# Attention steps of a head pair given to the next pair's stages from its first step on, and rope parts transposed ahead of the queries

## The chip, the cores and the metric

The kernel runs on one core of a Trainium2 chip. The metric is the device time of one execution in microseconds (us), and the time of a kernel is the median of several executions. The engines are named as in the profile: PE is TensorE (matmuls and transposes), PEld its weight loads, DVE is VectorE, ACT is ScalarE, POOL is GpSimd and SP is SyncE, which issues most DMAs.

## The reference

The program computes a two-layer encoder trunk on 512 tokens of width 1024: an mLSTM layer with a memory attention, then a multi-head latent attention layer (8 heads) with a memory attention. The change lies in the second layer. Cut to what matters:

```python
def shared_kv(...):                        # 8 heads, 128 plain + 64 rope columns
    c_kv, k_pe = split_cols(h @ w_kv_a, [KV_LORA, QK_ROPE])
    kv = (rmsnorm(c_kv, kv_lat_norm) @ w_kv_b).reshape(b, s, 8, 128 + 128)
    k = concat(kv[..., :128], broadcast(k_pe)); k = rmsnorm(k, k_gain)
    return concat(k[..., :128], rope(k[..., 128:])), kv[..., 128:]

def mla_layer(...):
    q = rmsnorm((rmsnorm(q_lat) @ w_q_up).reshape(b, s, 8, 192), q_gain)
    q = concat(q[..., :128], rope(q[..., 128:]))
    for j in range(4):                     # blocks of 128 queries
        sc = q_j @ k[: (j + 1) * 128].T * scale     # chunk-causal mask
        attn_j = softmax(sc) @ v[: (j + 1) * 128]
    y_b = attn * silu(z)                   # z: gate columns of h @ w_in
    return x + concat(y_b, y_mem) @ w_out
```

## The kernel before

Every product of two f32 operands is made of three matmuls on split operands: each operand is written as a high part and a low part (`split`, or in `load` for weights: ACT writes the high part at L130, DVE the rest at L131), and `prod` issues the high weight with both parts of the activation (L157), then the low weight with the high part (L162).

The second layer goes over four pairs of heads, p = 0 to 3. `b_pair(p)` is a generator of 14 steps, which are called m0 to m13 here:

- m0 to m3, `b_kv`: keys and values of token tile t0 to t3 (six matmuls of 512 columns each). DVE copies the keys out (L928), ACT the values.
- m4 to m7, `b_q`: queries of token tile t0 to t3 (nine matmuls of 384 columns each).
- m8 to m10 and m11 to m13, `b_z(p, 0)` and `b_z(p, 1)`: the gate of one head, in two halves of twelve matmuls of 512 columns, and a step with the SiLU (ACT tanh L200, DVE multiply L201). After each of these six steps `b_T` makes one transposed operand out of `todo`: k0, k1 (plain keys of head 0 and 1), q0, q1 (plain queries), kr, qr (the rope parts of both heads). Four PE transposes go into a PSUM tile `tp` (L952 for plain parts, L957 for rope parts). The high part is then written by ACT and the low part by DVE (L131 or L134 for plain parts; L960 and L963 for the rope parts, with a DVE cast L962 between them for the keys).

The tile `tp` is the one that all transposes share, and there are two of it:

```python
return pp.tile(list(shape), F32, tag="tp", bufs=2, name=nm("tp"))
```

The eight PSUM banks are 4 `acc`, 2 `att` and 2 `tp`. Weights have two buffers each of `wr`, `wh` and `wl`, so that a weight's split waits until the matmuls of the weight two loads earlier have read their buffer.

`b_attn(p)` is the attention of a pair, a generator of nine steps, n = 0 to 8. It goes over six units, u0 to u5: for each head the query blocks (0, 1) together, then block 2, then block 3. Step n issues the scores s of unit n (five matmuls for each block: L157 twice, L162, L1004, L1005), and the transposes t of unit n - 2 (L1018, into a `tp`, copied to the tile `e` by DVE at L1024 or, for block 2, by ACT at L1022). Steps 5 and 8 also issue the values of a head (20 matmuls at L1031) and its gated output (L346). Between scores and transposes lies the softmax on DVE and ACT (L328 to L341).

`weave(main, side, plan)` runs `main` and after its step i runs plan[i] steps of `side`. The attention of pair p runs as `side` beside the projections of pair p + 1; the attention of pair 3 runs beside the output projection. Pairs 0 and 1 are emitted in one order and then ordered on all engines by the framework's scheduler. The last `weave` (pairs 2 and 3, and the output projection) stands under `manual_schedule` for PE: there PE's order is that of the program, while the scheduler orders the other engines. Every engine goes through its own fixed list in order.

Of the kernel before, what the change touches and what calls it, by code (L numbers as in the profile page):

```python
# [40 lines left out]
def weave(main, side, plan=()):  # L41
    for i, _ in enumerate(main):
        for _ in range(plan[i] if i < len(plan) else 1):
            next(side, None)
    for _ in side:
        pass


def chain(*gens):
    for g in gens:  # L50
        yield from g
# [8 lines left out]
def trunk(ctx: ExitStack, tc: tile.TileContext, pv_d, pos_d, x_d, mem_d, memT_d, wmem_d, wg_d, wa_d, woa_d,  # L60
# [20 lines left out]
    def st(shape, tag, bufs=1, dt=F32):  # L81
        return POOLS.get(tag, sp).tile(shape, dt, tag=tag, bufs=bufs, name=nm(tag))
# [12 lines left out]
    def acc(shape=(P, 512)):  # L95
        return pp.tile(list(shape), F32, tag="acc", bufs=4, name=nm("acc"))

    def att(shape=(P, 512)):
        return pp.tile(list(shape), F32, tag="att", bufs=2, name=nm("att"))

    def tps(shape=(P, 512)):
        return pp.tile(list(shape), F32, tag="tp", bufs=2, name=nm("tp"))
# [46 lines left out]
    def prod(items, start, stop):  # L149

        left = {}
        for it in items:
            left[id(it[0])] = left.get(id(it[0]), 0) + 1
        seen = set()
        for ps, a_, w_, lhs in items:
            for x in a_:
                PE.matmul(ps, x if lhs else w_[0], w_[0] if lhs else x,  # L157
                          start=start and id(ps) not in seen, stop=False)
                seen.add(id(ps))
        for ps, a_, w_, lhs in items:  # L160
            left[id(ps)] -= 1
            PE.matmul(ps, a_[0] if lhs else w_[1], w_[1] if lhs else a_[0], start=False,  # L162
                      stop=stop and left[id(ps)] == 0)
# [159 lines left out]
    def softmax_rows(rows_, rq):  # L323

        n = len(rows_)
        mx = tiny([P, n])
        for j, ps in enumerate(rows_):
            V.tensor_reduce(mx[:, j:j + 1], ps, axis=AX.X, op=ALU.max)  # L328
        nb = tiny([P, n])
        V.scalar_tensor_tensor(out=nb, in0=mx, scalar=-1.0, in1=rq, op0=ALU.mult, op1=ALU.mult)  # L330
        pr = s2([P, 512])
        out = []
        sm = tiny([P, n])
        o = 0
        for j, ps in enumerate(rows_):
            out.append(pr[:, o:o + ps.shape[-1]])
            o += ps.shape[-1]
            A.activation(out[j], ps, AF.Exp, bias=nb[:, j:j + 1], scale=rq[:, j:j + 1], accum_out=sm[:, j:j + 1])  # L338
        V.reciprocal(sm, sm)
        for j in range(n):  # L340
            V.tensor_scalar(out[j], out[j], sm[:, j:j + 1], None, op0=ALU.mult)  # L341
        return out

    def gate_out(yT, row, ps, sz):
        y = s2()
        V.scalar_tensor_tensor(out=y, in0=ps, scalar=0.5, in1=sz, op0=ALU.mult, op1=ALU.mult)  # L346
        split(yT[0][:, row], yT[1][:, row], y)
# [557 lines left out]
    def b_z(p, c):  # L905
        d = pairs.setdefault(p, {})
        if c == 0:
            d["z"] = st([P, 2, S], ("z4", "mv")[p % 2])
        sz = d["z"]
        w = load(wb_d[8 + 2 * p + c], KT, P)  # L910
        ps = acc()
        yield from proj_T(w, hT, ps)
        silu2(sz[:, c], ps)
        yield

    def b_kv(p):
        d = pairs.setdefault(p, {})
        kns = st([P, NT, 256], "s4", 2)
        krs = s2([P, NT, P])
        d["v"] = vt = st([P, NT, 256], ("gt", "mkT")[p % 2])  # L920
        d["ks"] = kns, krs
        w = load(wkvb_d[p], 2, 512)
        ss = tiny([P, NT, 2])
        r2 = tiny([P, NT, 2])
        for t in range(NT):
            ps = acc()
            prod([(ps, lat(ckT, k, t), sub(w, slice(None), k), True) for k in range(2)], True, True)
            V.tensor_copy(kns[:, t], ps[:, 0:256])  # L928
            A.activation(vt[:, t], ps[:, 256:512], AF.Copy)
            for h in range(2):  # L930
                sqsum(kns[:, t, h * P:(h + 1) * P], ss[:, t, h:h + 1])
            if t < 3:
                yield
        V.tensor_tensor(out=ss, in0=ss, in1=sspe.unsqueeze(2).broadcast_to([P, NT, 2]), op=ALU.add)
        rpow(r2.rearrange("p a b -> p (a b)"), ss.rearrange("p a b -> p (a b)"), 1.0 / 192, EPS, 8)
        k4 = kns.rearrange("p t (h c) -> p t h c", h=2)
        V.tensor_tensor(out=k4, in0=k4, in1=r2.unsqueeze(3).broadcast_to([P, NT, 2, P]), op=ALU.mult)
        G.tensor_tensor(out=krs.rearrange("p t (h c) -> p t h c", h=2),
                        in0=kb.unsqueeze(2).broadcast_to([P, NT, 2, 64]),
                        in1=r2.unsqueeze(3).broadcast_to([P, NT, 2, 64]), op=ALU.mult)  # L940
        yield
# [48 lines left out]
    def b_attn(p):  # L990
        kn, qn, kh, qr, vt, sz, rqp = (pairs[p][n] for n in ("kn", "qn", "kr", "qr", "v", "z", "rq"))
        prs, pTs = {}, {}

        def scores(h, tiles):
            ps = acc() if p < 3 and tiles[0] == 2 else att()
            views = []
            for j, i in enumerate(tiles):
                n = (i + 1) * P
                m = max(n, 256)
                qs = slice(i * P, (i + 1) * P)  # L1000
                pt = ps[:, j * 256:j * 256 + m]
                prod([(pt, (qn[h][:, 0, qs], qn[h][:, 1, qs]), (kn[h][:, 0, :m], kn[h][:, 1, :m]), True)],
                     True, False)
                PE.matmul(pt, qr[:, h, qs], kh[:, h, :m], start=False, stop=False)  # L1004
                PE.matmul(pt, qr[:, h, qs], kl[:, h, :m], start=False, stop=True)  # L1005
                views.append(pt[:, :n])
            for v in views:
                V.memset(v[0:64, -64:], -1.0e30)
            prs[h, tiles] = softmax_rows(views, rqp[:, tiles[0]:tiles[-1] + 1, h])

        def trans(h, tiles):
            if tiles[0] == 0:
                pTs[h] = st([P, 1280], "e", 1)
            tp = tps()
            n = 0
            for i, pr in zip(tiles, prs[h, tiles]):
                for c in range(i + 1):
                    PE.transpose(tp[:, n:n + P], pr[:, c * P:(c + 1) * P], ident)  # L1018
                    n += P
            o = tiles[0] * (tiles[0] + 1) // 2 * P  # L1020
            if tiles[0] == 2:
                A.activation(pTs[h][:, o:o + n], tp[:, :n], AF.Copy)  # L1022
            else:
                V.tensor_copy(pTs[h][:, o:o + n], tp[:, :n])  # L1024

        def values(h):
            ps = att()
            for i in range(NT):
                for c in range(i + 1):
                    o = (i * (i + 1) // 2 + c) * P  # L1030
                    PE.matmul(ps[:, i * P:(i + 1) * P], vt[:, c, h * P:(h + 1) * P], pTs[h][:, o:o + P],  # L1031
                              start=c == 0, stop=c == i)
            gate_out(yT, 2 * p + h, ps, sz[:, h])

        units = [(h, tiles) for h in range(2) for tiles in ((0, 1), (2,), (3,))]
        lag = 2
        for n in range(len(units) + lag + 1):
            if n < len(units):
                scores(*units[n])
            if 0 <= n - lag < len(units):  # L1040
                trans(*units[n - lag])
            m = n - lag - 1
            if m >= 0 and m % 3 == 2:
                values(m // 3)
            yield

    def b_pair(p):
        yield from b_kv(p)
        yield from b_q(p)
        todo = [(n, h) for h in range(3) for n in "kq"]  # L1050
        for _ in chain(b_z(p, 0), b_z(p, 1)):
            yield
            b_T(p, *todo.pop(0))

    drain(b_pair(0))
    weave(b_pair(1), b_attn(0), (0,) * 5)
    x1b = []

    def residual():
        x1b.extend(load_x(x1_d, nc.sync))  # L1060
        yield from ()
# [5 lines left out]

    with tc.manual_schedule(engines={mybir.EngineType.PE}):
        weave(chain(*(b_pair(p) for p in range(2, 4)), residual(), out_proj(wob_d, yT, b_done)),
              chain(*(b_attn(p) for p in range(1, 4))), ((0,) * 5 + (1,) * 9) * 2)  # L1070


_OUTS = [((1, S, D), 'float32')]
# [101 lines left out]
```

## Time and profile before

| | |
|---|---|
| median of 3 runs | 769.12 us (769.11 to 769.58) |
| the profiled execution | 769.35 us, of which the traced span is 767.6 us |
| PE busy | 755.0 us, 98% of the span |
| PEld busy | 647.8 us, 84% |
| DVE busy | 484.1 us, 63% |
| ACT busy | 409.4 us, 53% |
| POOL busy | 106.8 us, 14% |

A share of busy time is an average over the whole span. Matmuls are pipelined and their ends are modelled, so that the duration of a row on PE is longer than the distance to the next row; the argument goes by the distances between starts. Pair 2 takes the stretch from 598.85 us of the span to 645.52, and pair 3 the one from 645.52 to 684.90; the output projection follows.

### The profile page before, as it was taken

To read this page: it belongs to the slowest core of one execution; us is meant where nothing else is said; L and a number is where in the kernel's file an instruction comes from. 1 tells how busy PE (TensorE), PEld (TensorE's weight loads), DVE (VectorE), ACT (ScalarE), POOL (GpSimd) and SP (SyncE) were. 2 spreads that over 40 slices of the span, in tenths; PEclk is the share of its full clock that TensorE was granted. 3 is DMA by queue.
4 is the path that set the end of the run, shared out by engine and by line. 5 is a ranking of instruction groups with operands and counts; after the bars stand their busy time and mean duration, and the time that the engine had idled before them with its cause. 6 is when DMAs were issued, how large, how long until landed. Compare 5 with 4: busy or idle time off the path is not lost.

```text
span 767.6 us, 10826 instructions
## 1 busy us (share of the span) xinstructions
PE 755.0 (98%) x3948; PEld 647.8 (84%) x3948; DVE 484.1 (63%) x945; ACT 409.4 (53%) x958; POOL 106.8 (14%) x159
## 2 busy tenths in 40 slices
PE   8999998999999999999999999999999999999998
PEld 6798887888888888888888887899888888888886
DVE  5743599547868836766434664566758697776422
ACT  6964557345446435536333658457856666644220
POOL 0131010010110101001001131020334230500000
PEclk9999999999999999999999999999999999999999
DMA  9523120322132222224443532121221111511241
GB/s 323 207 84 109 56 84 29 109 83 90 63 99 80 83 89 104 71 94 154 154 160 137 174 129 73 53 83 59 83 87 59 56 50 40 190 56 56 66 155 55
DMA packets 25909, 76.39 MB, mean 100 GB/s; under 512 B 3072, under 2 KB 3968, under 8 KB 25856
## 3 DMA queue, kind: packets, MB, share of 16 engines
q1 hardware_dynamic: 24144, 73.44, 28.4%
q10 hardware_dynamic: 1584, 2.25, 0.8%
q8 instruction: 31, 0.51, 0.3%
q14 instruction: 22, 0.18, 0.1%
q0 software_dynamic: 128, 0.01, 0.0%
HBM read 71.49 MB, written 4.19 MB: 99 GB/s over the span
## 4 chain that ended last, share of the span: by engine, by line
PE 85%; DVE 8%; ACT 3%; issue 1%; DMA 1%; POOL 0%; SPq 0%; ACTq 0%; DVEq 0%
PE acc L157 47%; PE acc L162 23%; PE att L157 3%; PE att L1031 2%; PE att L162 2%; DMA yTh<-in_wmem_dram 1%; DVE wl L131 1%; PE tp L1018 1%; DVE tiny L328 1%; ACT junk L187 1%; DVE kl L629 1%; ACT s L338 1%; PE tp L952 1%; PE att L715 1%; PE att L716 1%
## 5 line engine op out<-in xcount | busy, mean ns | idle before, releaser
L131 DVE TENSOR_TENSOR wl<-wr,wh 128x1024 fp32r<-128x1024 f32 (+5 forms) x117 | 136.2, 1165 | 152.9 <-ACT wh L130 126.7
L130 ACT ACTIVATE wh<-wr 128x1024 fp32r<-128x1024 f32 (+5 forms) x117 | 117.5, 1008 | 134.1 <-PE acc L157 123.8
L157 PE MATMUL acc<-wh,hTl 128*128 128x512 f32 (+3 forms) x320 | 113.3, 365 | 0.0
L157 PE MATMUL acc<-wh,hTh 128*128 128x512 f32 (+3 forms) x320 | 112.4, 367 | 0.3 <-ACT hTh L133 0.3
L157 PE MATMUL acc<-hTh,wh 128*128 128x512 f32 x256 | 101.8, 398 | 0.0
L157 PE MATMUL acc<-hTl,wh 128*128 128x512 f32 x256 | 100.3, 392 | 0.0
L157 PE MATMUL acc<-wh,yTh 128*128 128x512 f32 (+1 forms) x224 | 84.7, 382 | 0.0
L157 PE MATMUL acc<-wh,yTl 128*128 128x512 f32 (+1 forms) x224 | 84.5, 379 | 0.0
L162 PE MATMUL acc<-wl,hTh 128*128 128x512 f32 (+3 forms) x320 | 82.0, 364 | 0.0
L162 PE MATMUL acc<-hTh,wl 128*128 128x512 f32 x256 | 69.8, 392 | 0.0
L157 PEld LDWEIGHTS acc<-wh,hTh 128*128 128x128 f32 x320 | 59.1, 188 | 9.4 <-ACT hTh L133 0.6
L157 PEld LDWEIGHTS acc<-wh,hTl 128*128 128x128 f32 x320 | 59.6, 188 | 8.7 <-DVE hTl L134 0.2
L162 PEld LDWEIGHTS acc<-wl,hTh 128*128 128x128 f32 x320 | 56.5, 188 | 8.6
L162 PE MATMUL acc<-wl,yTh 128*128 128x512 f32 (+1 forms) x224 | 60.1, 378 | 0.0
L162 PEld LDWEIGHTS acc<-hTh,wl 128*128 128x128 f32 x256 | 47.6, 188 | 9.9 <-DVE wl L131 0.2
L157 PEld LDWEIGHTS acc<-hTh,wh 128*128 128x128 f32 x256 | 48.1, 188 | 9.1
L157 PEld LDWEIGHTS acc<-hTl,wh 128*128 128x128 f32 x256 | 48.2, 188 | 9.1
L157 PEld LDWEIGHTS acc<-wh,yTh 128*128 128x128 f32 x224 | 42.1, 188 | 7.2
L157 PEld LDWEIGHTS acc<-wh,yTl 128*128 128x128 f32 x224 | 42.1, 188 | 7.1
L162 PEld LDWEIGHTS acc<-wl,yTh 128*128 128x128 f32 x224 | 41.2, 188 | 7.4
L182 POOL TENSOR_SCALAR tiny<-tiny 128x8 f32<-128x8 f32 (+3 forms) x21 | 5.5, 262 | 245.1 <-ACT junk L187 68.2
L157 PE MATMUL acc<-wh,u 128*128 128x384 f32 (+1 forms) x160 | 37.8, 362 | 0.8 <-ACT u L133 0.7
(285 smaller groups left out, 1387.0 us busy)
## 6 DMA issues: line engine op xcount, KB each, us to landing
wr<-in_wa_dram SPq DMA_DIRECT2D x46, 512.0 KB, 3.2
wr<-in_wb_dram SPq DMA_DIRECT2D x16, 512.0 KB, 3.5
wr<-in_woa_dram SPq DMA_DIRECT2D x12, 512.0 KB, 3.2
wr<-in_wob_dram SPq DMA_DIRECT2D x12, 512.0 KB, 3.2
wr<-in_wmem_dram SPq DMA_DIRECT2D x8, 512.0 KB, 3.4
yTh<-in_wmem_dram SPq DMA_DIRECT2D x5, 512.0 KB, 7.3
yTl<-in_x_dram SPq DMA_DIRECT2D x4, 512.0 KB, 9.1
u<-in_x_dram SPq DMA_DIRECT2D x4, 512.0 KB, 6.2
```

What stands on the lines that cost most here:

```text
L130: A.activation(hi, src, AF.Copy)
L131: V.tensor_tensor(out=lo, in0=src, in1=hi.bitcast(F32), op=ALU.subtract)
L157: PE.matmul(ps, x if lhs else w_[0], w_[0] if lhs else x, start=start and id(ps) not in seen, stop=False)
L162: PE.matmul(ps, a_[0] if lhs else w_[1], w_[1] if lhs else a_[0], start=False, stop=stop and left[id(ps)] == 0)
L187: A.activation(j[:, :src.shape[-1]], src, AF.Square, scale=scale, accum_out=accum)
L328: V.tensor_reduce(mx[:, j:j + 1], ps, axis=AX.X, op=ALU.max)
L338: A.activation(out[j], ps, AF.Exp, bias=nb[:, j:j + 1], scale=rq[:, j:j + 1], accum_out=sm[:, j:j + 1])
L629: V.scalar_tensor_tensor(out=u[:, d:], in0=raw[:, :S - d], scalar=col("cw", (3 - d) * 16 + j), in1=u[:, d:], op0=ALU.mult, op1=ALU.add)
L715: PE.matmul(ps[:, :258], low(c, i), v[0][:, c], start=False, stop=False)
L716: PE.matmul(ps[:, :256], ph[:, blk(c, i)], v[1][:, c], start=False, stop=c == i)
L952: PE.transpose(tp[:, t * P:(t + 1) * P], main[:, t, h * P:(h + 1) * P], ident)
L1031: PE.matmul(ps[:, i * P:(i + 1) * P], vt[:, c, h * P:(h + 1) * P], pTs[h][:, o:o + P], start=c == 0, stop=c == i)
```

## The change

Two lines are changed. In all four pairs `b_T` takes its operands in another order: the rope parts kr and qr come third and fourth, ahead of both queries. For pairs 2 and 3 the plan of the last `weave` lets the attention of the pair before begin at m0 instead of m5: one step each after m0 to m4, m6, m8, m10 and m12, in place of one each after m5 to m13.

```diff
--- before.py
+++ after.py
@@ -1047,7 +1047,7 @@
     def b_pair(p):
         yield from b_kv(p)
         yield from b_q(p)
-        todo = [(n, h) for h in range(3) for n in "kq"]
+        todo = [("k", 0), ("k", 1), ("k", 2), ("q", 2), ("q", 0), ("q", 1)]
         for _ in chain(b_z(p, 0), b_z(p, 1)):
             yield
             b_T(p, *todo.pop(0))
@@ -1067,7 +1067,7 @@
 
     with tc.manual_schedule(engines={mybir.EngineType.PE}):
         weave(chain(*(b_pair(p) for p in range(2, 4)), residual(), out_proj(wob_d, yT, b_done)),
-              chain(*(b_attn(p) for p in range(1, 4))), ((0,) * 5 + (1,) * 9) * 2)
+              chain(*(b_attn(p) for p in range(1, 4))), (1, 1, 1, 1, 1, 0, 1, 0, 1, 0, 1, 0, 1, 0) * 2)
 
 
 _OUTS = [((1, S, D), 'float32')]
```

What stands on PE where pair 1 ends and pair 2 begins, before: the matmuls of the first key tile of pair 2 (`u4` are the latent's transposed tiles), then q1, the transposes of unit 5 of attention 0 and its values among kr and qr. The next row belongs to the queries of pair 2.

```order
L162 MATMUL acc_1096_5943<-wl_1084_5899,u4_877_5058 128x512 x2
L952 MATMUL tp_1069_5825<-ident_78,s4_997_5515 128x128 x4
L1018 MATMUL tp_1071_5845<-ident_78,s2_1056_5767 128x128 x4
L1031 MATMUL att_1075_5866<-e_1058_5772,gt_903_5155 128x128 x3
L957 MATMUL tp_1072_5851<-ident_78,s2_970_5434 128x128 x4
L1031 MATMUL att_1075_5866<-e_1058_5772,gt_903_5155 128x128 x4
L957 MATMUL tp_1077_5881<-ident_78,s2_998_5516 128x128 x4
L157 MATMUL acc_1110_5978<-wh_1102_5965,u4_895_5129 128x384
```

After the change, at the same place: the same first row, unit 4's transposes, qr (`tp_1069`), unit 5's transposes (`tp_1071`), q0 (`tp_1072`) and q1 (`tp_1077`), and then the first scores of attention 1.

```order
L162 MATMUL acc_1087_5904<-wl_1084_5899,u4_877_5058 128x512 x2
L1018 MATMUL tp_1068_5824<-ident_78,s2_1047_5734 128x128 x3
L1031 MATMUL att_1075_5868<-e_1058_5772,gt_903_5155 128x128 x3
L957 MATMUL tp_1069_5829<-ident_78,s2_998_5516 128x128 x4
L1031 MATMUL att_1075_5868<-e_1058_5772,gt_903_5155 128x128 x3
L1018 MATMUL tp_1071_5851<-ident_78,s2_1056_5767 128x128 x4
L952 MATMUL tp_1072_5857<-ident_78,s4_997_5515 128x128 x4
L1031 MATMUL att_1075_5868<-e_1058_5772,gt_903_5155 128x128 x4
L952 MATMUL tp_1077_5883<-ident_78,s4_997_5515 128x128 x4
L157 MATMUL att_1090_5917<-qk_1043_5704,qk_1073_5858 128x256 x2
```

Four operations with a `tp` stand behind one another there, with values between them, and q0 and q1 now lie right ahead of the scores that read them.

What DVE has at that place after the change, from the split of the next weight on: the casts and low parts of kr (from `tp_1062`), a gate multiply L201, a copy of keys L928, the low parts of qr (`tp_1069`), the copy of unit 5's transposes (`tp_1071`) and the low part of q0 (`tp_1072`).

```order
L131 TENSOR_TENSOR wl_1126_6059<-wr_1124_6056,wh_1125_6058 128x768
L962 COPY v_1063_5794<-v_1063_5794 64x512
L963 TENSOR_TENSOR kl_690_4136<-tp_1062_5793,v_1063_5794 64x512
L131 TENSOR_TENSOR yTl_629_3869<-s2_1061_5789,yTh_628_3868 128x512
L201 SCALAR_TENSOR_TENSOR mv_1031_5653<-s2_1074_5865,acc_1067_5811 128x512
L928 COPY s4_1079_5893<-acc_1087_5904 128x256
L962 COPY v_1063_5794<-v_1063_5794 64x512
L963 TENSOR_TENSOR kl_690_4136<-tp_1062_5793,v_1063_5794 64x512
L963 TENSOR_TENSOR v_1070_5830<-tp_1069_5829,v_1070_5830 64x512
L1024 COPY e_1058_5772<-tp_1071_5851 128x512
L963 TENSOR_TENSOR v_1070_5830<-tp_1069_5829,v_1070_5830 64x512
L131 TENSOR_TENSOR qk_1073_5858<-tp_1072_5857,qk_1073_5858 128x512
```

The low parts of kr stand behind a weight split, and the copy of unit 5's transposes behind them.

What stands on PE behind the first gate of pair 2 before: its last four matmuls, then scores and transposes of the attention and one transposed operand.

```order
L162 MATMUL acc_1145_6120<-hTh_626_3866,wl_1144_6117 128x512 x4
L157 MATMUL acc_1154_6183<-qk_1063_5794,qk_1070_5826 128x384 x2
L162 MATMUL acc_1154_6183<-qk_1063_5794,qk_1070_5826 128x384
L1004 MATMUL acc_1154_6183<-v_1073_5852,v_1078_5882 128x384
L1005 MATMUL acc_1154_6183<-kl_690_4136,v_1078_5882 128x384
L1018 MATMUL tp_1159_6199<-ident_78,s2_1136_6099 128x128 x4
L952 MATMUL tp_1160_6205<-ident_78,s4_1107_5975 128x128 x4
L157 MATMUL att_1163_6216<-qk_1063_5794,qk_1070_5826 128x512 x2
L162 MATMUL att_1163_6216<-qk_1063_5794,qk_1070_5826 128x512
```

After the change, at the same place: the same four matmuls, then k1 (`tp_1170`), unit 5's transposes (`tp_1173`), kr (`tp_1174`), and then the second gate.

```order
L162 MATMUL acc_1166_6209<-hTh_626_3866,wl_1165_6206 128x512 x4
L952 MATMUL tp_1170_6247<-ident_78,s4_1079_5893 128x128 x4
L1018 MATMUL tp_1173_6258<-ident_78,s2_1151_6152 128x128 x4
L957 MATMUL tp_1174_6264<-ident_78,s2_1080_5894 128x128 x4
L157 MATMUL acc_1179_6282<-hTh_626_3866,wh_1177_6278 128x512
```

Three operations with a `tp` stand directly behind one another, with no scores between them.

What DVE has for these three after the change: the split of the weight two loads on, the gate multiply, the copy of unit 5's transposes, the low part of k1, and the cast and low part of kr.

```order
L131 TENSOR_TENSOR wl_1194_6357<-wr_1192_6354,wh_1193_6356 128x1024
L201 SCALAR_TENSOR_TENSOR z4_1162_6202<-s2_1172_6255,acc_1166_6209 128x512
L1024 COPY e_1153_6157<-tp_1173_6258 128x512
L134 SCALAR_TENSOR_TENSOR qk_1171_6248<-tp_1170_6247,gg_112,qk_1171_6248 128x512
L962 COPY v_1175_6265<-v_1175_6265 64x512
L963 TENSOR_TENSOR kl_690_4136<-tp_1174_6264,v_1175_6265 64x512
```

The copy out of `tp_1173` stands behind a weight split and the gate multiply.

## Rows read from the trace of the kernel before

**Rows 1.** Stretches of pair 2 and the output projection: length, busy, clock, DMA.
```profile
core 0: us, PE busy (x) PEld busy (x) DVE busy (x) ACT busy (x) POOL busy (x), PEclk, DMA share, GB/s
598.85:645.52 46.67, 45.65 (x287) 40.44 (x286) 37.77 (x82) 29.08 (x82) 11.29 (x9) 1.00 0.18 53
...
723.00:761.00 38.00, 38.00 (x169) 31.48 (x169) 12.11 (x13) 7.00 (x7) 0.00 (x0) 1.00 0.25 83
```

**Rows 2.** Timeline of PE where it pauses in pairs 2 and 3.
```profile
start us, us, engine line op out<-in xcount [idle before <-releaser]
620.26 0.40 PE L1005 MATMUL att<-kl,v 128*128 128x512 f32 x1
620.74 0.70 PE L1018 MATMUL tp<-ident,s 128*128 128x128 f32 x3
...
625.11 0.28 PE L1005 MATMUL att<-kl,v 128*128 128x256 f32 x1
625.77 0.55 PE L1018 MATMUL tp<-ident,s 128*128 128x128 f32 x3 [0.38 <-DVE s L341]
...
632.00 0.39 PE L1005 MATMUL att<-kl,v 128*128 128x512 f32 x1
632.71 0.55 PE L1018 MATMUL tp<-ident,s 128*128 128x128 f32 x3 [0.32 <-DVE e L1024]
...
651.08 1.47 PE L157 MATMUL acc<-wh,u 128*128 128x384 f32 x6
652.38 0.51 PE L162 MATMUL acc<-wl,u 128*128 128x384 f32 x2
...
665.17 0.28 PE L1005 MATMUL att<-kl,v 128*128 128x256 f32 x1
665.63 0.55 PE L1018 MATMUL tp<-ident,s 128*128 128x128 f32 x3 [0.19 <-DVE s L341]
```

**Rows 3.** Timeline of DVE ahead of the third pause.
```profile
630.73 1.23 DVE L131 TENSOR_TENSOR wl<-wr,wh 128x1024 fp32r<-128x1024 f32 x1 [0.20 <-ACT wh L130]
...
631.99 0.67 DVE L1024 COPY e<-tp 128x512 f32<-128x512 f32 x1
```

**Rows 4.** Timeline of PE where pair 2 ends and pair 3 begins.
```profile
642.06 0.60 PE L1018 MATMUL tp<-ident,s 128*128 128x128 f32 x4
642.49 0.60 PE L957 MATMUL tp<-ident,s 128*128 128x128 f32 x4
642.93 2.40 PE L1031 MATMUL att<-e,mkT 128*128 128x128 f32 x20
645.16 0.60 PE L957 MATMUL tp<-ident,s 128*128 128x128 f32 x4
```

**Rows 5.** Timeline of DVE at the same place.
```profile
642.32 0.96 DVE L131 TENSOR_TENSOR wl<-wr,wh 128x768 fp32r<-128x768 f32 x1 [1.50 <-PE acc L162]
643.19 0.68 DVE L1024 COPY e<-tp 128x512 f32<-128x512 f32 x1
...
644.50 0.42 DVE L962 CAST v<-v 64x512 fp32r<-64x512 f32 x1
644.95 0.68 DVE L963 TENSOR_TENSOR kl<-tp,v 64x512 fp32r<-64x512 f32 x1
645.56 0.67 DVE L346 SCALAR_TENSOR_TENSOR s<-att,mv 128x512 f32<-128x512 f32 x1
...
648.51 0.68 DVE L131 TENSOR_TENSOR yTl<-s,yTh 128x512 fp32r<-128x512 f32 x1
649.11 0.42 DVE L928 COPY s<-acc 128x256 f32<-128x256 f32 x1
```

**Rows 6.** Timeline of DVE behind a gate of an earlier pair.
```profile
591.59 1.23 DVE L131 TENSOR_TENSOR wl<-wr,wh 128x1024 fp32r<-128x1024 f32 x1 [0.22 <-PE acc L162]
592.73 0.68 DVE L201 SCALAR_TENSOR_TENSOR mv<-s,acc 128x512 f32<-128x512 f32 x1
```

**Rows 7.** Timeline of ACT: a weight split and a split of transposed queries.
```profile
629.65 1.05 ACT L130 ACTIVATE wh<-wr 128x1024 fp32r<-128x1024 f32 x1
...
631.28 0.60 ACT L130 ACTIVATE qk<-tp 128x512 fp32r<-128x512 f32 x1 [0.58 <-PE tp L952]
```

**Rows 8.** Timeline of POOL: first and last of the rope of pair 3's queries.
```profile
662.62 0.99 POOL L872 TENSOR_TENSOR qt<-s,tabs 128x256 f32<-128x256 f32 x1 [5.10 <-ACT s L979]
...
668.68 1.32 POOL L875 TENSOR_TENSOR s<-s,qt 128x512 f32<-128x512 f32 x1
```

## The prediction

> **What bounds the kernel now.** The page's shares come first, then a table by stretch. In the stretch of pair 2 PE is busy for 45.65 of 46.67 us, DVE for 37.77 and ACT for 29.08, and the granted clock is 1.00 [rows 1]. PE is therefore the bound, and the only time that an order of the same work can win is PE's pauses. A busy row of PE is modelled, so pauses are read as distances between starts against the pace of PE where it waits for nothing: in the output projection 169 matmuls of 512 columns take 38.00 us, which is 0.225 each [rows 1]; 384 columns are 0.169 and 256 are 0.113 by the same pace. Four transposes take 642.49 - 642.06 = 0.43, so three take 0.32, and twenty value matmuls take 645.16 - 642.93 = 2.23, so 0.11 each [rows 4].
>
> The timeline of PE was then gone through, row against pace, over pairs 2 and 3. Five pauses stand out [rows 2]: 0.48 - 0.225 = 0.25 ahead of 620.74, 0.66 - 0.11 = 0.55 ahead of 625.77, 0.71 - 0.225 = 0.48 ahead of 632.71, 1.30 - 6 x 0.169 = 0.29 in the six matmuls from 651.08, and 0.46 - 0.11 = 0.35 ahead of 665.63. Together they are 1.9 us. Four of them are transposes of the attention that wait for the softmax or for a `tp`, and the change moves all of these to other stages.
>
> At this place a rule of the Trainium skill can be weighed. PEld is busy for 40.44 of the 46.67 us, 87% [rows 1]. The page "Perfetto Trace Analysis", section "Identifying the Most-Contended Engine", says that matmul busy time doesn't tell how near to its limit a kernel is, and that the busy share of the weight loads should be taken; by it about 13% of the stretch, 6 us, would be open. The trace doesn't agree: where PE runs without a pause PEld shows 31.48 of 38.00, 83% [rows 1], less than in pair 2. So 1.9 us is what can be won.
>
> **What one pause teaches.** The third of them shows the mechanism that the change meets again. The copy out of a `tp` stood on DVE behind a weight split: the split began at 630.73, the copy at 631.99, and it ended at 632.66 [rows 3]; PE's next transposes began at 632.71 [rows 2], 0.05 later. They waited for the `tp`, of which there are two. DVE can't pass the split, and the split can't begin before the matmuls that read its buffer are done: at the end of a gate it began 0.26 after the last of them (642.32 against 642.06) [rows 4, 5].
>
> **The change, part by part.** PE's work, its count and the list of DMAs on SP stay the same; a weight's DMA only waits for the split that frees its raw buffer, and shifts with it. What changes is how near operations with a `tp` stand to each other, and how much PE work lies between a producer and its reader.
>
> Removed: the five pauses, -1.9. Bounds -1.0 (the softmax pauses come back elsewhere) and -1.9.
>
> A, the end of pair 1 and the first key tile of pair 2. Let T be the start of that tile. PE then has six matmuls (1.35), unit 4's transposes (0.32), three values (0.33), qr (0.43), three values (0.33), and reaches unit 5's transposes at T + 2.76. Their `tp` is that of kr, whose last reader is the second L963 on DVE. Ahead of it DVE has, from T + 0.26 on, the 768-column split (0.87 to the next row), a cast (0.45), a low part (0.61), two operations of 512 columns (0.60 each, the distance from 648.51 to 649.11), a copy of 256 (0.42), and the cast (0.45) and low part (0.68) themselves [rows 5]: T + 4.94, with 0.05 for PE to start, T + 4.99. Unit 5's transposes wait for 2.2. They end at T + 5.42. The copy of them follows a low part of qr (4.94 + 0.61) and takes 0.68, to T + 6.23; q0, which needs a free `tp`, starts at 6.28 instead of 5.42 and waits for 0.9. q0's transposes end at 6.71; with 0.1 taken for the handing over, ACT writes the high part in 0.60 [rows 7] and DVE the low part in 0.68, to about 8.1. PE meanwhile has four values, q1 and one matmul of the first scores (0.45 + 0.43 + 0.11), is there at 7.7, and waits 0.4 for the low part. A = 3.5. Everything behind these on PE, the rest of the program, is late by as much. Lower bound 1.2: where DVE reads kr before it comes to the split, only the waits for q0 and its low part stay. Upper bound 4.1, with one more 512-column operation ahead.
>
> B, the first gate's start. Before, attention steps lay between the last query tile and the gate. Now the gate follows at once, and its weight split on ACT (1.05) [rows 7] waits for the fourth of that tile's nine matmuls, since the high weight of 768 columns is read till then. The other five last 0.85; with 0.05 to start the wait is 0.25, twice 0.5. Its relative is the pause at 651.08, 0.29 [rows 2]. Bounds 0 (the split on ACT isn't needed by then) and 0.5 each, with another ACT operation ahead.
>
> C, behind the first gate of pairs 2 and 3. Its end is E. k1, unit 5's transposes and kr stand directly behind one another; k1 and unit 5 take both `tp`, and kr should start at E + 0.86. On DVE the copy that frees the first stands behind the split of 1024 columns and the gate multiply: 0.26, then 1.14 (591.59 to 592.73), 0.60 for the multiply (0.68 long, followed after 0.60 as above) [rows 5, 6], and 0.68 for the copy: E + 2.68, PE at E + 2.73. kr waits for 1.9, in both pairs 3.7. Before, unit 5 had no such company: scores lay between the operands. Bounds 1.3 each (without the multiply) and 2.5 (one more operation of 512 columns).
>
> D, the softmax of unit 0. Between its scores and its transposes lay two query tiles and the scores of two units, 18 x 0.169 + 5 x 0.169 + 5 x 0.225 = 5.0 us, and the transposes waited 0.25 in pair 2 (620.74) and in pair 3 for nothing that can be read. Now two key tiles lie there, 12 x 0.225 instead of 18 x 0.169: 4.7. I take 0.3 for both pairs together; bounds 0 and 0.9.
>
> At no cost: the rope parts two steps earlier. In pair 3 the rope on POOL lasted from 662.62 to 670.00, 7.4 us [rows 8]. In the new order qr stands after the last query tile, two gate halves, k0, k1, two transposes, kr and a third half, about 3 x 2.7 + 2.0 = 10.1 us or 12 with C; ACT hands over the last rope copy some 2 us into that. The rope ends about 9.5 us in; with C gone the cover is under 1 us, and each us more on POOL would be on the path. The end of pair 2 and of pair 3 is covered: there q0 and q1 have a gate half each before them. Pairs 0 and 1 are ordered by the scheduler on PE too; 0, bounds -0.3 and 0.7.
>
> The sum: 769.35 (profiled) + 3.5 + 0.5 + 3.7 + 0.3 - 1.9 = 775.4. The profiled execution lies 0.23 over the median; on the scale of the median it is **775.2 us**.
>
> **The rivals.** First, faster. The pauses go, and the new neighbours cost nothing: 769.12 - 1.9 = 767.2. It is so if the copy of unit 5 ends within 0.8 us of the first gate's end, that is if it passes the split, and if kr is read before T + 2.7. For it: DVE has 8.9 us free in the stretch of pair 2 [rows 1], and the attention's softmax is spread more evenly. Against it: DVE's fixed list, where both stand behind a split. The Trainium skill, page "Perfetto Trace Analysis", section "Optimization Strategy", speaks for this rival, since it says that interleaving stretches with different bounds may help; no stretch read here has a bound other than PE. Chance 0.07.
>
> Second, no change, 767.6 to 770.7 (0.2% to either side is about what a measurement can tell). A at 1.2 and C at half of its lower bound would be 1.2 + 1.3 + 0.5 - 1.9 = 1.1 more, 770.2. It needs DVE to reach the split later than its place in the list, with the `tp` readers done. Chance 0.13.
>
> Third, slower by more. The new order of operands holds in pairs 0 and 1 too; if kr waits behind their first gates as in pairs 2 and 3, that is 3.7 more, 778.9. Against it: the scheduler can put other work on PE there. Chance 0.08. That the change does nothing is ruled out, since the order of PE differs as shown.
>
> **How the numbers follow.** The forecast, a loss from waits for `tp` between about 771 and 778.2, has 0.72. The upper end is 775.2 and 3: C at 2.5 each is 1.3 more, A 0.6, B 0.5, D 0.6. The lower end takes A and C at their lower bounds, 775.2 - 2.3 - 1.1 - 0.5 = 771.3. Leaving out the first and third rival (0.15) and the faster part of the second (0.05), the range is 769.3 to 778.2. Faster 0.07, same 0.13, slower 0.72 + 0.08 = 0.80.
>
> **What would show it.** In the changed profile: L957 behind the first gates of pairs 2 and 3 with an idle time of 1.3 to 2 us whose releaser is DVE L1024; L1018 behind the first key tile of pair 2 idle for about 2 us with releaser DVE L963, and L952 behind it with L1024; the first L157 of the gate idle for some 0.25 with ACT L130; none of the five old pauses; PE's busy time and the clock as before. The prediction is wrong if kr starts directly behind unit 5's transposes, if the order on DVE in time lets the copy run ahead of the split, or if the softmax in the key stage takes so long that the transposes of the later units wait by more than 1 us.

## The result, and the profile after

The changed kernel takes 776.43 us in the median (775.40 to 777.58, four executions), against 769.35 (769.11 to 769.82) for the kernel before beside it. The ratio is 1.0092, with an interval from 1.0080 to 1.0104: slower by 0.9%. Forecast were 775.2 us and a range of 769.3 to 778.2.

The profiled execution took 775.91 us, with a span of 774.1, which is 6.5 more than before. The page's first part shows that no engine has more to do; PE is busy 1.0 us longer, and where its clock was lower is shown below:

```profile
PE 756.0 (98%) x3948; PEld 649.2 (84%) x3948; DVE 482.9 (62%) x945; ACT 409.5 (53%) x958; POOL 106.6 (14%) x159
```

**Behind the first gate of pair 2.** The timeline of PE (start, length, work, idle time before it and its releaser), where before scores lay between the operands:

```profile
635.42 1.07 PE L162 MATMUL acc<-hTh,wl 128*128 128x512 f32 x4
636.34 0.60 PE L952 MATMUL tp<-ident,s 128*128 128x128 f32 x4
636.77 0.60 PE L1018 MATMUL tp<-ident,s 128*128 128x128 f32 x4
639.28 0.67 PE L957 MATMUL tp<-ident,s 128*128 128x128 f32 x4 [1.91 <-DVE e L1024]
```

and that of DVE at the same place, to be read beside [rows 6] and [rows 3]:

```profile
636.72 1.22 DVE L131 TENSOR_TENSOR wl<-wr,wh 128x1024 fp32r<-128x1024 f32 x1 [1.47 <-ACT wh L130]
637.86 0.68 DVE L201 SCALAR_TENSOR_TENSOR z<-s,acc 128x512 f32<-128x512 f32 x1
638.46 0.68 DVE L1024 COPY e<-tp 128x512 f32<-128x512 f32 x1
```

k1 (L952) and unit 5 (L1018) have taken both `tp`. Waits are given here as the distance between starts less PE's pace; the idle time in a row's bracket is shorter, because a row's modelled length reaches into it. kr (L957) could have begun at 637.20 and begins at 639.28, 0.14 after the copy out of unit 5's tile ends at 639.14. The copy was ready to go at about 637.3, and DVE was busy with the split and the gate multiply, which stand ahead of it. In pair 3 unit 5's transposes start at 679.55, and kr waits for 2.18:

```profile
682.16 0.63 PE L957 MATMUL tp<-ident,s 128*128 128x128 f32 x4 [2.01 <-DVE e L1024]
```

**Where pair 1 ends.** PE from the first key tile of pair 2 on:

```profile
600.03 1.09 PE L157 MATMUL acc<-wh,u 128*128 128x512 f32 x4
600.96 0.62 PE L162 MATMUL acc<-wl,u 128*128 128x512 f32 x2
601.42 0.49 PE L1018 MATMUL tp<-ident,s 128*128 128x128 f32 x3
601.74 0.83 PE L1031 MATMUL att<-e,gt 128*128 128x128 f32 x6
602.64 0.63 PE L957 MATMUL tp<-ident,s 128*128 128x128 f32 x4
603.10 0.83 PE L1031 MATMUL att<-e,gt 128*128 128x128 f32 x6
605.14 0.66 PE L1018 MATMUL tp<-ident,s 128*128 128x128 f32 x4 [1.21 <-DVE kl L963]
606.58 0.66 PE L952 MATMUL tp<-ident,s 128*128 128x128 f32 x4 [0.78 <-DVE e L1024]
```

DVE there, with the low parts of kr as the first and the fourth row shown, of which the second ends at 605.08, 0.06 ahead of PE's row at 605.14; before, the same kinds of work took as long [rows 5]:

```profile
601.71 0.68 DVE L963 TENSOR_TENSOR kl<-tp,v 64x512 fp32r<-64x512 f32 x1
602.32 0.67 DVE L131 TENSOR_TENSOR yTl<-s,yTh 128x512 fp32r<-128x512 f32 x1
...
603.96 0.42 DVE L962 CAST v<-v 64x512 fp32r<-64x512 f32 x1
604.39 0.69 DVE L963 TENSOR_TENSOR kl<-tp,v 64x512 fp32r<-64x512 f32 x1
```

**The first gates' start.** PE in pair 2; pair 3 has the same at 672.73:

```profile
628.99 0.68 PE L162 MATMUL acc<-wl,u 128*128 128x384 f32 x3
629.95 0.50 PE L157 MATMUL acc<-hTh,wh 128*128 128x512 f32 x1 [0.27 <-ACT wh L130]
```

**The clock.** In stretches of 2 us behind the wait of pair 2 (the same columns as in [rows 1]; the granted clock is the third figure from the end):

```profile
638.00:640.00 2.00, 0.71 (x5) 0.75 (x6) 1.80 (x3) 0.01 (x1) 1.07 (x1) 0.94 0.36 98
640.00:642.00 2.00, 2.00 (x6) 1.52 (x6) 1.10 (x2) 0.80 (x2) 0.00 (x0) 0.50 0.00 0
642.00:644.00 2.00, 2.00 (x8) 1.58 (x7) 1.12 (x2) 0.37 (x1) 0.00 (x0) 0.71 0.00 0
644.00:646.00 2.00, 2.00 (x13) 1.64 (x11) 0.65 (x1) 0.59 (x1) 0.00 (x0) 1.00 0.00 0
```

It is 0.50 after the wait, the lower of PE's two levels (1.2 GHz), and PE's matmuls of 512 columns stand 0.43 apart there:

```profile
640.18 0.63 PE L157 MATMUL acc<-hTl,wh 128*128 128x512 f32 x1
640.60 0.63 PE L157 MATMUL acc<-hTh,wh 128*128 128x512 f32 x1
641.03 0.63 PE L157 MATMUL acc<-hTl,wh 128*128 128x512 f32 x1
```

The eight of them from 639.67 to 643.16 take 3.49 us. The same eight in pair 3, behind the same kind of wait and at 1.00, take 1.93 (682.55 to 684.48). The low clock thus cost 1.6 us.

### The profile page after: what moved, and what is told of

Read it like the earlier page. It is cut to its first block, busy times and chain, and to the rows that moved or that the text cites. A ratio compares the mean times of both kernels' runs of the same rounds, so it can differ in the third digit from the quotient of the medians.

```text
span 774.1 us, 10832 instructions
## 1 busy us (share of the span) xinstructions
PE 756.0 (98%) x3948; PEld 649.2 (84%) x3948; DVE 482.9 (62%) x945; ACT 409.5 (53%) x958; POOL 106.6 (14%) x159
## 4 chain that ended last, share of the span: by engine, by line
PE 86%; DVE 7%; ACT 3%; DMA 2%; issue 1%; POOL 0%; SPq 0%; ACTq 0%; DVEq 0%
PE acc L157 48%; PE acc L162 23%; PE att L157 4%; PE att L1031 2%; PE att L162 2%; DVE wl L131 1%; PE tp L1018 1%; DMA yTh<-in_wmem_dram 1%; ACT wh L130 1%; DVE kl L629 1%; DVE tiny L328 1%; PE tp L952 1%; ACT junk L187 1%; PE att L715 1%; PE att L716 1%
```

## Experiments

Each was timed beside the kernel before. The first four shared a chip, and so did the next four and the last three. Where a row shown stands at the edge of its view, the count behind the x can be lower than the program's.

**The plan alone** (the old order of the operands comes back):

```diff
-        todo = [("k", 0), ("k", 1), ("k", 2), ("q", 2), ("q", 0), ("q", 1)]
+        todo = [(n, h) for h in range(3) for n in "kq"]
```

> The new plan with the old order of the operands (k0, q0, k1, q1, kr, qr). Theory of the shared transpose buffers: behind the first gate of pairs 2 and 3 now stand q0, unit 5's transposes and k1, so the same copy of unit 5 stands behind the same weight split and k1 waits about 2.1 us in each pair, with the low clock behind the first of them; and since kr and qr are now made last, the first scores of attention 1 and 2 wait for their low parts, about 2 us each. So slower than the changed kernel, 777 to 781 us. Rival, that the early rope parts are what costs: then the old order cures it, k1 starts at once and the time is under 772 us.

777.86 us (777.17 to 778.87), ratio 1.0109 (1.0091 to 1.0127). The wait behind the first gates is there without kr: k1 stands in its place.

```profile
641.42 0.44 PE L952 MATMUL tp<-ident,s 128*128 128x128 f32 x2 [1.82 <-DVE e L1024]
```

And the scores wait for the rope parts, which are now made last, at the end of pair 1 and of pair 2:

```profile
610.97 0.38 PE L1004 MATMUL att<-v,v 128*128 128x256 f32 x1 [1.69 <-DVE v L963]
...
654.12 0.39 PE L1004 MATMUL att<-v,v 128*128 128x256 f32 x1 [1.26 <-DVE v L963]
```

By the distances these waits are 1.85 and 1.42. So the plan carries the loss. That the new order of the operands repairs a part of it isn't shown by the times, since the intervals of the two ratios (1.0109 and 1.0092) overlap. The traces show what it saves: the 1.42 at the end of pair 2. At the end of pair 1 PE waits as long in both (0.38 + 0.72 + 1.85 here, 2.9 in the changed kernel).

**The order of the operands alone** (the old plan comes back):

```diff
-              chain(*(b_attn(p) for p in range(1, 4))), (1, 1, 1, 1, 1, 0, 1, 0, 1, 0, 1, 0, 1, 0) * 2)
+              chain(*(b_attn(p) for p in range(1, 4))), ((0,) * 5 + (1,) * 9) * 2)
```

> The new order of the operands with the old plan. Theory: the loss comes from where the attention's transposes lie, so this stays with the kernel before, 768.5 to 770.5 us, its pauses in the query stages of pairs 2 and 3 still there (1.6 us) and no pause of 2 us behind a first gate. Rival, that the rope parts ahead of the queries cost by themselves: 771 us or more, with L957 waiting behind a gate.

770.39 us (770.08 to 771.64), ratio 1.0014 (1.0004 to 1.0023). It lies within the expected range but not at no change. L957 does wait behind the gate, for an ACT copy, in both pairs, by 0.90 us: a small form of the same wait. Here unit 4's transposes stand ahead of the rope part.

```profile
637.67 0.49 PE L1018 MATMUL tp<-ident,s 128*128 128x128 f32 x3
638.89 0.30 PE L957 MATMUL tp<-ident,s 128*128 128x128 f32 x1 [0.73 <-ACT e L1022]
```

The longest wait lies at the end of pair 1, where q0 stands directly behind unit 5's transposes and waits 1.23 us for their copy:

```profile
609.39 0.66 PE L952 MATMUL tp<-ident,s 128*128 128x128 f32 x4 [1.05 <-DVE e L1024]
```

Of the old pauses, which were expected to stay with 1.6 us, 0.6 is left (0.20 ahead of 631.86 and 0.36 ahead of 665.46). So the new order has a price of its own, about 0.1%, and waits for a `tp` are in it too.

**kr in another PSUM tile.** The changed kernel, with kr's transposes in one of the four `acc`:

```diff
-        tp = tps()
+        tp = acc() if (name, h) == ("k", 2) else tps()
         if h < 2:
```

> The changed kernel with one edit: kr's four transposes go into a PSUM tile of the kind acc, of which the gate stage uses few, and not into one of the two tp. DVE's work, its place in the lists and the plan stay. Theory: kr then starts behind unit 5's transposes without a wait (2.1 us gone in each of pairs 2 and 3), the granted clock stays at 1.00 behind it (1.7 us gone), and unit 5 of attention 0 no longer waits for kr's last reader (1.4 us gone): 776.4 - 4.2 - 1.7 - 1.4 = 769.1, with 768.3 to 771 taken. Rival, that DVE's load is the limit and the buffer only the place where it shows: the wait goes to the next transposes or the first scores, and the time stays over 774 us.

767.66 us (767.09 to 769.18), ratio 0.9979 (0.9969 to 0.9988): faster than both, and 0.6 below the expected range. PE behind the first gate of pair 2:

```profile
634.08 0.60 PE L952 MATMUL tp<-ident,s 128*128 128x128 f32 x4
634.51 0.60 PE L1018 MATMUL tp<-ident,s 128*128 128x128 f32 x4
634.95 0.60 PE L957 MATMUL acc<-ident,s 128*128 128x128 f32 x4
635.31 0.48 PE L157 MATMUL acc<-hTh,wh 128*128 128x512 f32 x1
```

DVE is as late as in the changed kernel:

```profile
634.46 1.22 DVE L131 TENSOR_TENSOR wl<-wr,wh 128x1024 fp32r<-128x1024 f32 x1 [1.47 <-ACT wh L130]
635.60 0.68 DVE L201 SCALAR_TENSOR_TENSOR z<-s,acc 128x512 f32<-128x512 f32 x1
636.20 0.68 DVE L1024 COPY e<-tp 128x512 f32<-128x512 f32 x1
```

The copy begins 2.12 us after the gate's end in both (638.46 - 636.34; 636.20 - 634.08), and kr starts without a wait. So DVE's lateness by itself cost nothing here; what cost was that PE needed the tile that DVE had still to empty. The waits for kr's readers at the end of pair 1 are gone too. Left there are 0.36 for a `tp` and 0.43 for the low part of q0, where the changed kernel has 1.01 and 0.30, and qr's 0.23 is gone as well; the theory had taken off 1.4 there and no more.

**Unit 5 later.** The changed kernel, with unit 5's transposes behind the third gate half:

```diff
-(1, 1, 1, 1, 1, 0, 1, 0, 1, 0, 1, 0, 1, 0) * 2
+(1, 1, 1, 1, 1, 0, 1, 0, 1, 0, 0, 1, 1, 0) * 2
```

> The changed kernel with the plan's last steps moved: unit 5's transposes follow the first half of the second gate and no longer stand between k1 and kr. Theory: the waits of 2.1 us behind the first gates and the low clock go (5.9 us), the waits at the end of pair 1 (2.9 us) stay, and qr, which now stands behind unit 5 with kr's tp still being read, waits up to 0.7 us in each pair: 776.4 - 5.9 + 0 to 1.4 = 770.5 to 772. Rival, that the plan's early steps are what costs, wherever unit 5 stands: over 774 us.

772.70 us (771.68 to 773.87), ratio 1.0043 (1.0027 to 1.0059), a little over the expected end. kr starts without a wait. A wait half as long, 1.04 in pair 2 and 1.05 in pair 3, turns up where unit 5 now stands ahead of qr; up to 0.7 was expected. The granted clock of the profile is 1.00 in both pairs. The end of pair 1 is as in the changed kernel (1.37 and 1.01).

```profile
640.21 0.60 PE L1018 MATMUL tp<-ident,s 128*128 128x128 f32 x4
641.68 0.30 PE L957 MATMUL tp<-ident,s 128*128 128x128 f32 x1 [0.87 <-DVE e L1024]
```

**The copy on ACT.** The changed kernel, with the copies of units 2 and 5 on ACT:

```diff
-            if tiles[0] == 2:
+            if tiles[0] >= 2:
                 A.activation(pTs[h][:, o:o + n], tp[:, :n], AF.Copy)
```

> The changed kernel with the copy of the transposes of query block 3 (unit 2 and unit 5) on ACT and no longer on DVE; buffers and plan stay. Theory: what holds kr is the copy's place behind DVE's weight split and gate multiply. On ACT it stands behind the high half of the same split, the tanh and the high part of k1, and ends some 2 us after the gate's end, so that kr waits for 1.2 us in each pair and no longer for 2.1: 1.8 us less than the changed kernel, 774.6, and 773 if the granted clock then stays up. Rival, that the wait is for something else (the softmax or kr's own source): the wait of 2.1 us stays and the time is 776 or more.

772.29 us (771.94 to 772.46), ratio 1.0036 (1.0023 to 1.0050). kr waits for 1.17 us in each pair, as worked out, now for ACT, and the granted clock of the profile stays at 1.00 in both pairs. The time is 0.7 below the 773 expected for that. Of this the trace shows a part: unit 0's wait of 0.17 is gone, and kr's waits fell by 1.9 in all. At the end of pair 1 unit 5 waits less (1.02) and q0 more (1.53, for ACT), so that nothing is won there. The rest wasn't traced.

```profile
636.30 0.60 PE L1018 MATMUL tp<-ident,s 128*128 128x128 f32 x4
637.90 0.30 PE L957 MATMUL tp<-ident,s 128*128 128x128 f32 x1 [1.00 <-ACT e L1022]
```

**The buffer without the change.** The kernel before, with the edit of kr_in_acc:

> The kernel before with kr's transposes in a PSUM tile of the kind acc; old order of operands, old plan. It tells whether the gain of kr_in_acc is the buffer's alone. Theory: before, kr had a tp in time but for one wait of 0.37 us at the end of pair 1, so this gains at most that: 768.7 to 769.4 us; the pauses of the softmax (1.6 us) stay, and the new plan is what removes them. Rival, that the buffer alone is the gain: 767.7 us or less.

770.08 us (769.74 to 771.64), ratio 1.0006 (0.9998 to 1.0015): no gain, and not the small one that was expected. At the end of pair 1, where the framework ordered things anew, the waits grew, 0.79 us at a L957 for DVE and 0.64 at the first query tile for ACT (0.37 and 0.20 before), and of the softmax's pauses, expected to stay, 0.5 is left. From 590 us of the span on PE's pauses together are 0.3 us shorter than before, and ahead of that, where the edit holds as well, 1.1 us longer. The gain of kr_in_acc is thus not had by the buffer alone.

**The gate's split covered.** kr in `acc`, and the attention's sixth step after the last query tile:

```diff
-(1, 1, 1, 1, 1, 0, 1, 0, 1, 0, 1, 0, 1, 0) * 2
+(1, 1, 1, 1, 1, 0, 0, 1, 1, 0, 1, 0, 1, 0) * 2
```

> kr in a PSUM tile of the kind acc, as in kr_in_acc, and the attention's sixth step given after the last query tile and no longer after the third, so that scores, transposes and values lie between the last query tile and the first gate, whose weight split on ACT starts late. Theory of that split: the two waits of 0.43 us at the first gate's start go, 767.7 - 0.9 = 766.8 us, with 766.3 to 767.3 taken. Rival: the transposes of that step or unit 5's softmax come too late in the new place and the time stays at 767.7 or more.

767.88 us (766.39 to 768.81), ratio 0.9973 (0.9961 to 0.9984). Of seven executions three lie at 766.4 to 766.5 and four at 767.9 to 768.8, so this median settled nothing against kr_in_acc. In the profile, that of the slowest of them, the waits at the first gates' start are gone, and the granted clock fell once in the first layer (0.73 between 128 and 132 us of the span). That doesn't explain the group, since its other three show a mean granted clock of 1.000.

**The changed kernel again, for its clock:**

> The changed kernel once more, for its granted clock. Theory: the stretch at the lower level behind a wait of 2.1 us comes and goes from one execution to the next and is worth 1.7 us each time; so executions between 775 and 778 us, and this profile has either none, one or two of these stretches, and its span goes with their number: 772.4, 774.1 or 775.8 us. Rival, that it belongs to that place: again one stretch behind the first gate of pair 2 alone.

776.55 us (776.12 to 777.20). The profile, with a span of 775.4, has two stretches at the lower clock: one behind the first gate of pair 2, as before, and one behind the waits at the end of pair 1, where there was none before.

```profile
606.00:610.00 4.00, 3.21 (x19) 3.19 (x19) 2.80 (x5) 1.61 (x4) 0.00 (x0) 0.67 0.00 0
640.70:645.70 5.00, 5.00 (x18) 4.04 (x19) 2.73 (x5) 1.18 (x2) 0.00 (x0) 0.66 0.08 29
```

Pair 3 had the same wait (2.09 us) and no low clock. At pair 1's end the low clock came in one of two profiles, as the theory has it; behind the gate of pair 2 it came in both, as the rival has it. That each stretch is worth 1.7 us doesn't hold: the one at pair 1's end lengthened its rows by about 1 us.

**Three on one chip.** First kr_in_acc again:

> kr_in_acc again, beside the next two on one chip: 767.7 us, as measured before, with the two waits of 0.43 us at the first gates' start.

767.81 us (767.49 to 769.31), ratio 0.9977 (0.9968 to 0.9986).

> kr_acc_gate_cover again, beside kr_in_acc on one chip. Theory: its executions without a low clock stand 0.9 us under those of kr_in_acc, 766.4 to 766.8 us. Rival: the sixth step's new place costs as much as the gate's wait, and both medians are the same within 0.3 us.

766.34 us (766.15 to 767.18), ratio 0.9960 (0.9947 to 0.9972): the lowest median of this study, 1.5 under kr_in_acc beside it. The first measurement of the same kernel, with its 767.88, didn't show this gain, so the size of it isn't settled. The covered split was to bring 0.9; where the other 0.6 came from wasn't traced. The gate starts as soon as the values are done; their twenty rows take 2.23 us [rows 4], and the gate's first row stands 2.16 behind the first of them.

```profile
625.50 2.40 PE L1031 MATMUL att<-e,mkT 128*128 128x128 f32 x20
627.66 0.48 PE L157 MATMUL acc<-hTh,wh 128*128 128x512 f32 x1
627.97 0.39 PE L157 MATMUL acc<-hTl,wh 128*128 128x512 f32 x1
```

Then one edit more, the attention beginning one step later:

```diff
-(1, 1, 1, 1, 1, 0, 0, 1, 1, 0, 1, 0, 1, 0) * 2
+(0, 1, 1, 1, 1, 1, 0, 1, 1, 0, 1, 0, 1, 0) * 2
```

> As kr_acc_gate_cover, but with the attention beginning after the second step of the pair (0, 1, 1, 1, 1, 1, 0, 1, 1, ...), so that a second key tile lies between the last transposes of pair 1 and the first scores. Theory: the waits there for a tp and for the low part of q0 (0.36 and 0.43 us, in pair 2 alone) go, and 766.4 - 0.8 = 765.6 to 766.6 us is left. Rival: the softmax of the first units then comes too late in the query stage, as in the kernel before, and pauses of 0.3 to 0.5 us come back there, 766.8 us or more.

767.77 us (767.42 to 769.80), ratio 0.9978 (0.9969 to 0.9986). The rival had it: the wait for a `tp` at pair 1's end goes (0.36; that for q0 stays with 0.31), and transposes of the query stage wait in both pairs, 0.72 and 1.13. The profile names L1008 on DVE, which runs there directly behind the softmax's last step (L341, 619.13 to 619.61).

```profile
619.76 0.41 PE L1018 MATMUL tp<-ident,s 128*128 128x128 f32 x2 [0.56 <-DVE acc L1008]
...
659.48 0.30 PE L1018 MATMUL tp<-ident,s 128*128 128x128 f32 x1 [0.96 <-DVE acc L1008]
```

## Why the prediction was right, and where its terms were off

The mechanism was right: transposes close together run out of the two `tp`, because the engine that empties a tile stands behind a weight split that begins only behind the gate's end. kr_in_acc shows it by taking away the need for the tile while DVE is as late as before, copy_on_act by having the tile emptied sooner, with a wait shorter by as much. The Trainium skill, page "Perfetto Trace Analysis", section "Optimization Strategy", says that a gap which repeats on the engine that should be full can mean that there is too little PSUM for the next tile; the runs agree, the gap of 2.1 us in each pair going to nothing once kr has a tile of another kind.

**C** was forecast with 1.9 us a pair and measured 2.08 and 2.18. The split started 0.38 and 0.47 after the gate's end, not 0.26, and PE 0.14 after the copy, not 0.05. What the split waited for was not the gate's last matmul, as the prediction has it, but its high half on ACT. That takes 1.06 and began 0.20 after PE had gone on to the low weight (635.42), in pair 3 0.29 after it (678.21), where the profile names the DMA of the weight:

```profile
635.62 1.06 ACT L130 ACTIVATE wh<-wr 128x1024 fp32r<-128x1024 f32 x1 [1.16 <-PE acc L157]
678.50 1.06 ACT L130 ACTIVATE wh<-wr 128x1024 fp32r<-128x1024 f32 x1 [1.25 <-DMA wr<-in_wob_dram]
```

So the size came out nearly right, but by another path than the one forecast.

**A** was forecast with 3.5 and measured 0.23 (qr) + 1.37 (unit 5) + 1.01 (q0) + 0.30 (q0's low part) = 2.9. The forecast instant on DVE was nearly met: unit 5's transposes started 5.11 after T, forecast 4.99. Off was PE's own way there. The term "three values (0.33)" was mis-sized: the trace has two records for each value matmul that the order lists, the values of one head being ten rows of the order and twenty records, so that three of them take 0.67. PE came later by twice 0.33 and waited less. The 20 matmuls that the section on the kernel before gives for the values of a head are likewise records; the program has ten. The term "four values" (0.45) ahead of the first scores took 0.89 for the same reason; a wait of 0.30 was left there because q0's low part came late too, 8.56 after T and not 8.1.

**B** was forecast with 0.25 each and measured 0.44: the split on ACT began at 628.84, 0.20 after the start of the query tile's fifth matmul (628.64), and not at once.

**D** came to 0.17 in pair 2 (614.35 to 614.75, less 0.227), with nothing in pair 3 that can be read, against 0.3.

**Removed:** of the five pauses [rows 2] none is left at its place. The pace was taken there as 0.225 for 512 columns, which counts 1.9; by the 0.227 of PE's longer runs it is the same. Left out of the sum were two short waits at the end of pair 1, 0.37 ahead of L957 (608.94) and 0.20 ahead of the query tile (610.93), which went too.

**The clock** had no term. The prediction expected it to be as before. It added 1.6 us in the profiled execution. Too small in the forecast were this (nothing), B and C; too large was A, by 0.6, and the two waits that also went, 0.6, were left out. The forecast terms add up to 6.1 and the span grew by 6.5, so the near agreement of the sum is in part luck: errors of opposite sign. Of the four executions one, 775.40, has a mean granted clock of 1.000; it wasn't the profiled one.

The measured terms are 2.9 + 4.26 + 0.88 + 0.17 + 1.6 - 1.9 - 0.6 = 7.3, against 6.5 in the span. Of the difference 0.5 lies ahead of pair 2: its first key tile starts 1.18 later than before, but PE has by then done 1.64 us more of pair 1's leftovers. The rest, 0.3, is spread over differences below 0.15 and wasn't traced.

One more sentence ahead of the prediction was wrong. The rows shown of PE before at the end of pair 1 begin with the fourth key tile of pair 2, not with its first: before, the leftovers of pair 1 lay among all four key tiles, and DVE had that much longer for kr. After the change they have to be done behind the first key tile, because the first scores of the attention stand there. The rows of after were described rightly, and the steps of A, which rest on them, stand.

The first rival (faster, 767.2) failed: the copy of unit 5 didn't pass the split. A time near it was reached only once kr had a tile of another kind, with 767.7. The second (no change) fell with A and C. The third, the same wait behind the gates of pairs 0 and 1, didn't happen: pair 2 began only 1.18 us later with 1.64 us more work done.

Still open is why a wait of about 2.1 us was followed by a low clock in pair 2 twice and in pair 3 never in two profiles, and why the executions of kr_acc_gate_cover fell into two groups.

## What to carry to other kernels

Before spreading side work into other stages, count for each new neighbourhood how many tiles of the shared buffer are asked for in a row, and read from the releasing engine's list what stands ahead of each release; a long operation there that waits for the bounding engine itself can turn into a stall, as the split did here. A buffer kind with tiles to spare in that stage is the cheap remedy: here one `acc` turned a loss of 0.9% into a gain of 0.2%, and with a step that covers the next weight split the gain was 0.4% in one measurement and 0.3% in another. Where one edit of a pair seems to be at fault, run each alone: here the operands' order, which looked like the risk, cost 0.1% alone and, by the traces, took 1.4 us off what the plan cost.

## What the runs showed of the hardware that was not expected

A wait of about 2 us on PE, in a kernel that shows a granted clock of 1.00 nearly everywhere, can be followed by a granted clock of 0.50, in which matmuls of 512 columns stand 0.43 us apart instead of 0.23; eight of them took 3.49 us instead of 1.93. It need not: in the two profiles of the changed kernel it came behind the wait of pair 2 both times (2.08 and 2.09 us), behind that of pair 3 (2.18 and 2.09) not at all, and behind those of pair 1's end once. In the profile of plan_only, with waits of 1.99 and 2.00 in the same places, the clock of the execution was 1.00. And in the profile of kr_acc_gate_cover it fell once in the first layer (0.73 between 128 and 132 us), where no single wait ahead of it was over 1 us.
